# A hybrid attention block: q, k, v order, second q and k buffers, eight staging tiles for y and product banks for the turned probabilities in its differential heads

## The chip, the cores and the metric

The kernel runs on one core of a Trainium2 chip. The metric is the device time of one execution in microseconds (us); the median of the runs is given, beside the time of each. Five engines work side by side, each through its own queue of instructions in order: TensorE (PE in the profile; PEld is its weight load), VectorE (DVE), ScalarE (ACT), GpSimd (POOL) and SyncE (SP). SyncE issues most of the transfers, GpSimd some.

## The reference

One layer on 512 tokens and 16 learned ones ahead of them, width 1024, all in float32. Two attentions read the same normed input: a stick-breaking one with 8 heads of 128, and a differential one with 8 heads that have two maps of 64 each. Their outputs are projected, merged by gates, projected again and followed by a SwiGLU.

```python
def diff_attn_block(q, k, v, lam, slopes, qpos, kpos, qcid, kcid):
    s = jnp.einsum('bhcqd,bhckd->bhcqk', q, k).astype(jnp.float32) * (DF_HEAD_DIM ** -0.5)
    ...
    s = jnp.where(mask, s + bias[None, :, None], -jnp.inf)
    p = jax.nn.softmax(s, axis=-1)
    w = p[:, :, 0] - lam * p[:, :, 1]
    return jnp.einsum('bhqk,bhkd->bhqd', w.astype(v.dtype), v)
...
        y_sb = o_sb @ w_br_sb[l]
        y_df = o_df @ w_br_df[l]
        gates = jax.nn.sigmoid(xn @ w_gate[l] + b_gate[l]).reshape(B, L_pad, 2, D)
        merged = gates[:, :, 0] * y_sb + gates[:, :, 1] * y_df
        h = h + merged @ w_out[l]
```

## The kernel before

**Products.** Each float32 operand is split into a high part and a low part, and each product is three matmuls: high by high, high by low, low by high (L227, L228, L229, in `mm3`). The normed input lies transposed on chip as xT_h and xT_l. Results collect in PSUM: two tiles of two banks under the tag z (`z_tile`, L63) and four single banks under the tag mm (`mm_tile` and `tr_tile`, L57 and L60), which go round among the projections, y, the turns of v and the norm of a head.

**Weights.** They come in blocks of 512 KB. The list `stream` (L78 to L117) fixes their order; `stage_one` (L128) issues the load of the next block on SyncE into one of three staging tiles `wst` (L141, L144), and `split` (L74) makes the high part `wh` on ScalarE (L75) and the low part `wl` on VectorE (L76). `weights` (L215) prepares as many blocks ahead as `READY` says (3) in the stick-breaking heads and 2 later; `at_of["df", 0, 2]` marks where that changes.

**The heads.** The main loop (L921 to L955) runs 8 stick-breaking heads, then 8 differential ones. Each head is a generator that issues its scores, maps, turns and weighted values, and at each `yield n` the loop puts in up to n units of other work: projections of the next head, and the product `y` of a finished pair of heads with the branch's output weights. A y unit makes two of y's eight blocks (L711), twelve matmuls of 512 columns. The units of a head are those of its successor, then the first y unit, the turn of the successor's v (L462 to L478), and the second y unit. The scheduler places the instructions of these pieces by priority; evacuations and the last steps of a map carry a raised one (`EVAC`).

**A differential head** (`df_head`, L622). `scores` and `scores3` write two maps at a time to a z tile (L632, L633); VectorE adds the bias and takes the maximum (L636), ScalarE exponentiates (L660), VectorE normalises and subtracts the second map (L663 to L666), which leaves `pr`. Then `attn_out` (L482) turns the probabilities with transposes (L493, L507, L510), copies them out as a_h, a_l, a_f and a_s (L495, L496, L511, L514), and `weighted` multiplies by v ("av" below, L516 to L525). The result is copied off z (L690); its norm (L695) is left for the next head.

**q and k of a differential head** (`df_units`, L594). Both have one buffer per part, under the tags qh, ql, kh and kl. The evacuation splits each half of the partitions into its high and low parts (L604, L605 for q, L611, L612 for k), and for k two transfers on GpSimd's queue (L615) copy the finished half to the other partitions, 264 KB each. The units of a head run v, q, k (L618), and its weights come in that order too (L93).

**y and its way home.** Each y block is copied from its bank by ScalarE (L725) to a staging tile `ys`, one of two of that name alternately with `sg` tiles, or, for the last pair of differential heads, the tiles of the maps (L718 to L723), and stored in device memory by GpSimd, for a branch's first pair plainly, after that with addition (L727, L729). At the end `y_back` (L974) loads the sums on SyncE, and GpSimd multiplies them by the gates (L991).

**Shared memory.** The stick-breaking heads from the third on use token sums, in tA and tB. tA lies in the pool xtp under the tag y_sb; the residual rows `hres` (L997, four loads of 512 KB on GpSimd's queue, L999) use the same tag, so they may be loaded once tA was last read. tB lies in opool under the tag y_df.

Of the kernel before, what the change touches and what calls it, by code (L numbers as in the profile page):

```python
# [9 lines left out]
F32 = mybir.dt.float32  # L10
F32R = mybir.dt.float32r
# [5 lines left out]
P = 128  # L17
D = 1024
SEQ = 512
NM = 16  # L20
L = NM + SEQ
KT = D // P
# [13 lines left out]
STAGE, READY, START = 5, 3, 4  # L36
# [4 lines left out]
def block_kernel(ctx: ExitStack, tc: tile.TileContext, x, meta, norm_mix_g, w_in, w_gate, b_gate,  # L41
# [18 lines left out]
    def tr_tile():  # L60
        return ps_mm.tile([P, 512], F32, tag="mm", name="tr")

    def z_tile():  # L63
        return ps_z.tile([P, 2, 512], F32, tag="z", name="z")
# [25 lines left out]
        if h > 2:  # L90
            rows(("y_sb", h - 3), w_br_sb, (h + 1) % 2 * 512, (h - 3) // 2 * 2)
    for h in range(NH):
        for i in (2, 0, 1):  # L93
            cols(("df", h, i), w_in, (3 + i) * D + h * P)
        if h < 3:
            rows(("y_sb", h + 5), w_br_sb, (h + 1) % 2 * 512, (h + 5) // 2 * 2)
        else:
            rows(("y_df", h - 3), w_br_df, (h + 1) % 2 * 512, (h - 3) // 2 * 2)
# [20 lines left out]
    at_of = {c[0]: n for n, c in enumerate(stream)}  # L119
# [95 lines left out]
    def weights(key):  # L215
        at = at_of[key]
        if at < START:
            return loaded[key]
        if at >= first_ffn:
            return fpools["down"](key)  # L220
        prepare(prep_at[key] + (READY if at < at_of["df", 0, 2] else 2))
        return loaded[key]

    def mm3(ps, pairs, start=True, stop=True, skip=False):
# [42 lines left out]
    xT = (xT_h, xT_l)  # L267

    ydram = ctx.enter_context(tc.tile_pool(name="ydram", bufs=1, space=bass.MemoryType.DRAM))
    y_count = [0]  # L270

    tA = xtp.tile([P, 2, 2, 4, HL], F32R, tag="y_sb", name="tA")
    y_part = {n: [ydram.tile([P, SEQ], F32, name=f"{n}_{f}") for f in range(KT)] for n in ("y_sb", "y_df")}
# [205 lines left out]

        return kv_units(key, lambda ps, s: nc.scalar.copy(vT[:, s], ps)), turn  # L480

    def attn_out(blocks, d, lo_rows):  # L482

        qn = P - lo_rows
        off = (0, 512, 896)
        a_h = ap_.tile([P, 1152], F32R, tag="a_h", name="a_h")
        a_l = ap_.tile([P, 1152], F32R, tag="a_l", name="a_l")
        a_f = ap_.tile([P, P], F32, tag="a_f", name="a_f")

        def turn(j, pt):  # L490
            n = 512 - j * P
            for t in range(j, NQ):
                nc.tensor.transpose(pt[:, (t - j) * P:(t - j + 1) * P], blocks(t, j * P, (j + 1) * P), ident)  # L493
            c = slice(off[j], off[j] + n)
            nc.scalar.copy(a_h[:, c], pt[:, 0:n])  # L495
            nc.vector.tensor_tensor(a_l[:, c], pt[:, 0:n], a_h[:, c].bitcast(F32), op=ALU.subtract)  # L496

        def turn_first():
            z = z_tile()
            turn(0, z[:, 0])  # L500
            turn(1, z[:, 1])

        def turn_rest():
            z = z_tile()
            turn(2, z[:, 0])
            pt = z[:, 1]
            nc.tensor.transpose(pt[:, 384:512], blocks(3, 3 * P, 4 * P), ident)  # L507
            for t in range(NQ):
                b = blocks(t, (t + 1) * P - 32 * t, (t + 1) * P + NM)
                nc.tensor.transpose(pt[0:32 * t + NM, t * qn:(t + 1) * qn], b[lo_rows:P], ident[lo_rows:P, lo_rows:P])  # L510
            nc.scalar.copy(a_f, pt[:, 384:512])  # L511
            for t in range(NQ):
                r, c = slice(32 * t, 32 * t + NM), slice(t * qn, (t + 1) * qn)
                (nc.scalar.copy if t < 2 else nc.vector.tensor_copy)(a_s[r, c], pt[r, c])  # L514

        def weighted():  # L516
            vf, vh, vl = d["v"]
            ps = z_tile()[:, 0]
            for j in range(3):
                n = 512 - j * P  # L520
                mm3(ps[:, j * P:512], [(vh[:, j], vl[:, j], a_h[:, off[j]:off[j] + n], a_l[:, off[j]:off[j] + n])], j == 0, False)
            nc.tensor.matmul(ps[:, 3 * P:512], lhsT=vf[:, 0], rhs=a_f, start=False, stop=False)
            nc.tensor.matmul(ps.rearrange("p (t q) -> p t q", q=P)[:, :, lo_rows:P], lhsT=vf[:, 1],
                             rhs=a_s[:, 0:4 * qn], start=False, stop=True)
            return ps  # L525

        return turn_first, turn_rest, weighted
# [22 lines left out]
    def sb_head(h, d, o_h, o_l):  # L550
        qh, ql = d["q"]
        kh, kl = d["k"]
        zA, zB = z_tile(), z_tile()

        def score(o, t, k0, k1, mo, mn):
            q = slice(t * P, (t + 1) * P)
            mm3(o, [(qh[:, q], ql[:, q], kh[:, k0:k1], kl[:, k0:k1])], stop=(mn == 0))
            if mn:
                nc.tensor.matmul(o[:, mo:mo + mn], lhsT=ident_b, rhs=mask_b[:, 0:mn], start=False, stop=True)

        score(zA[:, 0, 0:256], 0, 0, 256, NM, P)
        score(zA[:, 0, 144:416], 1, 0, 272, NM + P, P)
        score(zA[:, 1, 0:416], 2, 0, 416, NM + 2 * P, 144)
        score(zB[:, 0, 0:HL], 3, 0, HL, 0, 0)
        score(zB[:, 1, 0:HL], 3, HL, L, 400 - HL, P)
        res = []
        for z, n in ((zA, 416), (zB, HL)):
            zz = z[:, :, 0:n]
            e = ap_.tile([P, 2, n], F32, tag=("w2" if n == 416 else "w1"), name="e")
            s = ap_.tile([P, 2, n], F32, tag=("w3" if n == 416 else "w0"), name="s")  # L570
            nc.scalar.activation(e, zz, AF.Abs)
            nc.scalar.activation(e, e, AF.Exp, scale=-1.0)
            nc.scalar.activation(e, e, AF.Ln, bias=1.0)
            nc.vector.scalar_tensor_tensor(s, zz, 0.0, e, op0=ALU.max, op1=ALU.add)
            sf = s.rearrange("p a b -> p (a b)")
            for a, b in (((0, 144), (144, 416), (416, 832)) if n == 416 else ((0, L),)):
                f = sf[:, a:b][:, ::-1]
                nc.vector.tensor_tensor_scan(f, f, f, 0.0, op0=ALU.add, op1=ALU.bypass)  # L578
            nc.vector.tensor_tensor(s, zz, s, op=ALU.subtract)
            nc.scalar.activation(s, s, AF.Exp)  # L580
            res.append(sf)
        base = ((0, 0), (0, 144), (0, 416), (1, 0))
        t1, t2, av = attn_out(lambda t, k0, k1: res[base[t][0]][:, base[t][1] + k0:base[t][1] + k1], d, 96)
        yield 4 if h + 1 < SEVEN else 5
        t1()
        yield 1
        t2()
        yield 1
        ps = av()
        nc.scalar.copy(o_h, ps)  # L590
        nc.vector.tensor_tensor(o_l, ps, o_h.bitcast(F32), op=ALU.subtract)


    def df_units(h):  # L594
        d = {}
        hs = (slice(0, 64), slice(64, 128))
        q = [ap_.tile([P, SEQ], F32R, tag=("qh", "ql")[c], name=f"dq{c}") for c in range(2)]
        k = [ap_.tile([P, 2, L], F32R, tag=("kh", "kl")[c], name=f"dk{c}") for c in range(2)]
        d["q"], d["k"] = q, k

        def q_evac(ps):
            for c in range(2):
                a, b = hs[c], hs[1 - c]
                nc.scalar.activation(q[c][a], ps[a], AF.Copy, scale=DF_SCALE)  # L604
                nc.vector.scalar_tensor_tensor(q[c][b], ps[a], DF_SCALE, q[c][a].bitcast(F32),  # L605
                                               op0=ALU.mult, op1=ALU.subtract)

        def k_evac(ps, s, scale):
            for c in range(2):
                a = hs[c]  # L610
                nc.scalar.activation(k[c][a, 0, s], ps[a], AF.Copy, scale=scale)  # L611
                nc.vector.scalar_tensor_tensor(k[c][a, 1, s], ps[a], scale, k[c][a, 0, s].bitcast(F32),  # L612
                                               op0=ALU.mult, op1=ALU.subtract)
                if s.stop == L:
                    nc.gpsimd.dma_start(k[c][hs[1 - c]].bitcast(F32), k[c][a].bitcast(F32))  # L615

        kv, turn = kv_all("df", h, k_evac, d)
        return d, kv[2:4] + halves(("df", h, 0), xT, QT, q_evac) + kv[0:2], turn  # L618

    late = []  # L620

    def df_head(h, d, o_h, o_l):  # L622
# [53 lines left out]
        yield 1  # L676
        scores3(1)
        maps(3)
        t1, t2, av = attn_out(lambda t, k0, k1: prs[t][:, 0, k0:k1], d, 64)
        yield 3 if h < NH - 1 else 2  # L680
        t1()
        yield 1
        t2()
        yield 2
        ps = av()
        of = ap_.tile([P, SEQ], F32, tag="of", name="of")
        sq = ap_.tile([P, SEQ], F32, tag="sq", name="sq")
# [21 lines left out]
    def y_units(name, i, o):  # L709

        def unit(fs):  # L711
            wh, wl = weights((name, i))
            for f in fs:
                ps = mm_tile()
                cs = slice(f % 4 * P, (f % 4 + 1) * P)
                mm3(ps, [(wh[:, k, cs], wl[:, k, cs], o[0][:, k], o[1][:, k]) for k in range(2)])

                if name == "y_df" and i > 5:  # L718
                    ys = ap_.tile([P, SEQ], F32, tag=f"w{y_count[0] % 4}", name="ys")
                elif y_count[0] % 2:  # L720
                    ys = ap_.tile([P, SEQ], F32, tag="ys", bufs=2, name="ys")
                else:
                    ys = gate_tile(0)  # L723
# [197 lines left out]
    for br in range(2):  # L921
        name, head = (("y_sb", sb_head), ("y_df", df_head))[br]
        if br:
            nc.gpsimd.memset(a_s, 0.0)
        for h in range(NH):
            if (br, h) == (0, 0):
                tB["t"] = opool.tile([P, 2, 2, 4, HL], F32R, tag="y_df", name="tB", bufs=1)
# [363 lines left out]
```

## Time and profile before

| | us |
|---|---|
| runs | 997.58, 999.05, 1001.49 |
| median | 999.05 |
| the profiled execution | 1000.49 |
| its span in the trace | 998.6 |
| TensorE busy | 970.5 (97%) |
| VectorE busy | 687.9 (69%) |
| ScalarE busy | 572.2 (57%) |
| GpSimd busy | 158.2 (16%) |

The mean granted TensorE clock is 0.993 of full speed. The rows shown further on have these forms. A wait: engine, tile and line, what it waited for, us in total, times, longest. A stretch: from and to, its length, busy time and instructions of PE, PEld, DVE, ACT and POOL, the granted clock, the busy share of the DMA engines, GB/s. A row of the timeline: start, duration, engine, line, operation, result and operands, count, and in brackets the idle time before it and what ended it. A group: line, engine, operation, count, busy us, mean ns of one. An issue of a transfer: count, KB, us from issue to landing.

### The profile page before, as it was taken

How to read it: one execution, taken by the hardware profiler on the slowest of the kernel's cores; microseconds unless marked ns; L12 is line 12 of the kernel's file. 1: busy time of each engine (PE TensorE's matmuls, PEld its weight loads, DVE VectorE, ACT ScalarE, POOL GpSimd, SP SyncE). 2: the span in 40 equal slices, each digit the busy share in tenths (PEclk: the TensorE clock that was granted, in tenths of full speed). 3: DMA queues.
4: the chain of work that ended last, by engine and by line, in shares of the span. 5: the costliest groups of instructions: out<-in, count | busy, mean ns of one | idle time of the engine just before them, and what ended most of it. 6: DMA issues, size and time to landing. Idle time of an engine off the chain costs nothing.

```text
span 998.6 us, 16211 instructions
## 1 busy us (share of the span) xinstructions
PE 970.5 (97%) x6213; PEld 870.4 (87%) x6213; DVE 687.9 (69%) x1244; ACT 572.2 (57%) x1091; POOL 158.2 (16%) x216
## 2 busy tenths in 40 slices
PE   7999999989999999999999999989999999999996
PEld 5998888879888998889878888879999999988885
DVE  8998678764567777678632633798888888754544
ACT  5676766665566666666772533575555555643533
POOL 4010112121232222322314530000000000000103
PEclk9999999998999999999999999999999999999999
DMA  7312444465563444643838732223343434332212
GB/s 214 86 43 65 127 131 96 97 190 127 127 142 105 93 129 128 148 109 92 161 84 209 223 117 85 85 78 114 94 118 94 119 90 122 100 112 99 92 43 85
DMA packets 140241, 114.12 MB, mean 114 GB/s; under 512 B 4962, under 2 KB 115715, under 8 KB 140163
## 3 DMA queue, kind: packets, MB, share of 16 engines
q1 hardware_dynamic: 129810, 89.29, 29.7%
q0 software_dynamic: 10192, 23.73, 11.9%
q8 instruction: 49, 0.80, 0.3%
q14 instruction: 30, 0.24, 0.1%
q10 hardware_dynamic: 160, 0.07, 0.0%
HBM read 89.87 MB, written 18.87 MB: 109 GB/s over the span
## 4 chain that ended last, share of the span: by engine, by line
PE 78%; DVE 8%; ACT 6%; DMA 5%; issue 2%; POOL 1%; SPq 0%; DVEq 0%; POOLq 0%; ACTq 0%
PE mm L229 18%; PE mm L227 18%; PE mm L228 18%; PE z L227 6%; PE z L229 6%; PE z L228 6%; DMA dk<-dk 3%; PE z L493 1%; ACT wh L75 1%; PE z L632 1%; DVE wl L76 1%; PE z L633 1%; DMA wst<-in_w_in_dram 1%; DVE s L578 1%; DMA xs<-in_x_dram 1%
## 5 line engine op out<-in xcount | busy, mean ns | idle before, releaser
L76 DVE TENSOR_TENSOR wl<-wst,wh 128x1024 fp32r<-128x1024 f32 (+1 forms) x150 | 170.0, 1137 | 118.9 <-ACT wh L75 118.7
L228 PE MATMUL mm<-xT_l,wh 128*128 128x264 f32 (+2 forms) x656 | 213.7, 326 | 2.2 <-DVE xT_l L828 2.2
L227 PE MATMUL mm<-xT_h,wh 128*128 128x264 f32 (+2 forms) x656 | 214.6, 327 | 0.6 <-ACT xT_h L827 0.6
L229 PE MATMUL mm<-xT_h,wl 128*128 128x264 f32 (+2 forms) x656 | 213.5, 325 | 0.0
L75 ACT CAST wh<-wst 128x1024 fp32r<-128x1024 f32 (+1 forms) x150 | 145.8, 972 | 98.9 <-PE mm L228 40.4
L228 PEld LDWEIGHTS mm<-xT_l,wh 128*128 128x128 f32 x656 | 124.2, 189 | 11.6 <-DVE xT_l L828 2.4
L227 PEld LDWEIGHTS mm<-xT_h,wh 128*128 128x128 f32 x656 | 124.4, 190 | 10.3 <-ACT xT_h L827 1.1
L229 PEld LDWEIGHTS mm<-xT_h,wl 128*128 128x128 f32 x656 | 124.1, 189 | 9.8
L228 PE MATMUL mm<-hT_l,wh 128*128 128x256 f32 x284 | 80.5, 284 | 0.7 <-DVE hT_l L1074 0.7
L227 PE MATMUL mm<-hT_h,wh 128*128 128x256 f32 x284 | 80.2, 284 | 0.6 <-DVE sg L1169 0.6
L229 PE MATMUL mm<-hT_h,wl 128*128 128x256 f32 x284 | 80.1, 283 | 0.0
L660 ACT ACTIVATE pr<-pr,nm 128x144 f32<-128x144 f32 (+3 forms) x64 | 36.3, 568 | 40.4 <-DVE nm L658 40.4
L228 PEld LDWEIGHTS mm<-hT_l,wh 128*128 128x128 f32 x284 | 53.7, 189 | 1.2 <-DVE hT_l L1074 1.1
L227 PEld LDWEIGHTS mm<-hT_h,wh 128*128 128x128 f32 x284 | 53.4, 189 | 1.1 <-DVE sg L1169 0.7
L229 PEld LDWEIGHTS mm<-hT_h,wl 128*128 128x128 f32 x284 | 53.6, 189 | 0.0
L227 PE MATMUL mm<-o_h,wh 128*128 128x512 f32 x128 | 52.3, 410 | 0.3 <-ACT o_h L703 0.3
L229 PE MATMUL mm<-o_h,wl 128*128 128x512 f32 x128 | 51.6, 404 | 0.0
L228 PE MATMUL mm<-o_l,wh 128*128 128x512 f32 x128 | 50.0, 392 | 0.0
L227 PE MATMUL mm<-t_h,wh 128*128 128x256 f32 x168 | 47.4, 282 | 1.3 <-ACT wh L75 1.0
L228 PE MATMUL mm<-t_l,wh 128*128 128x256 f32 x168 | 47.3, 281 | 1.1 <-DVE t_l L1089 1.1
L475 POOL COPY v_s<-vT 128x16 f32<-128x16 f32 x64 | 17.8, 307 | 190.6 <-ACT vT L480 82.3
L229 PE MATMUL mm<-t_h,wl 128*128 128x256 f32 x168 | 47.3, 281 | 0.0
(314 smaller groups left out, 2508.0 us busy)
## 6 DMA issues: line engine op xcount, KB each, us to landing
wst<-in_w_in_dram SPq DMA_DIRECT2D x40, 512.0 KB, 4.1
wst<-in_w_ffn_gate_dram SPq DMA_DIRECT2D x22, 512.0 KB, 3.7
wst<-in_w_ffn_down_dram SPq DMA_DIRECT2D x22, 512.0 KB, 3.5
wsu<-in_w_ffn_up_dram SPq DMA_DIRECT2D x21, 512.0 KB, 3.8
wst<-in_w_gate_dram SPq DMA_DIRECT2D x16, 512.0 KB, 4.6
y_df<-ys POOLq DMA_DIRECT2D x20, 256.0 KB, 6.2
dk<-dk POOLq DMA_DIRECT2D x16, 264.0 KB, 5.8
wst<-in_w_br_sb_dram SPq DMA_DIRECT2D x8, 512.0 KB, 4.9
```

What stands on the lines that cost most here:

```text
L75: (hi_copy or nc.scalar.copy)(hi, src)
L76: (lo_eng or nc.vector).tensor_tensor(lo, src, hi.bitcast(F32), op=ALU.subtract)
L227: nc.tensor.matmul(ps, lhsT=ah, rhs=bh, start=(start and i == 0), stop=False, skip_group_check=skip)
L228: nc.tensor.matmul(ps, lhsT=ah, rhs=bl, start=False, stop=False, skip_group_check=skip)
L229: nc.tensor.matmul(ps, lhsT=al, rhs=bh, start=False, stop=(stop and i == n - 1), skip_group_check=skip)
L475: nc.gpsimd.tensor_copy(v_s[:, 32 * t:32 * t + NM], vT[:, (t + 1) * P:(t + 1) * P + NM])
L493: nc.tensor.transpose(pt[:, (t - j) * P:(t - j + 1) * P], blocks(t, j * P, (j + 1) * P), ident)
L578: nc.vector.tensor_tensor_scan(f, f, f, 0.0, op0=ALU.add, op1=ALU.bypass)
L632: nc.tensor.matmul(o, lhsT=q[c][:, qs], rhs=k[c][:, 0, k0:k1], start=True, stop=False)
L633: nc.tensor.matmul(o, lhsT=q[c][:, qs], rhs=k[c][:, 1, k0:k1], start=False, stop=True)
L660: nc.scalar.activation(pr[:, c], pr[:, c], AF.Exp, bias=nm[:, c:c + 1], accum_out=ls[:, t, c:c + 1])
```

## The change

1. **Order.** The weights of a differential head are streamed as q, k, v, and its units run q, k, v. The mark in `weights` moves to the first block of the differential branch.
2. **Second q and k.** Odd heads hold q and k in one tile `dqk` in tB's memory; even heads keep the old tags.
3. **Staging for y.** From the first differential head on, y goes through the eight slots of one tile `y_out` in tA's memory. `hres` has the same tag, so its loads now come behind the last store out of `y_out`.
4. **Turned probabilities.** `attn_out` is given its banks. Stick-breaking heads pass the two halves of a z tile as before; differential heads pass two mm banks for each of the two turns.
5. **Units.** The last yield of a differential head ahead of av is 1 where it was 2, so the second y unit comes behind av.

```diff
-        for i in (2, 0, 1):
+        for i in range(3):
             cols(("df", h, i), w_in, (3 + i) * D + h * P)
...
-        prepare(prep_at[key] + (READY if at < at_of["df", 0, 2] else 2))
+        prepare(prep_at[key] + (READY if at < at_of["df", 0, 0] else 2))
...
-    def attn_out(blocks, d, lo_rows):
+    def attn_out(blocks, d, lo_rows, banks):
...
         def turn_first():
-            z = z_tile()
-            turn(0, z[:, 0])
-            turn(1, z[:, 1])
+            for j, pt in enumerate(banks()):
+                turn(j, pt)
 
         def turn_rest():
-            z = z_tile()
-            turn(2, z[:, 0])
-            pt = z[:, 1]
+            p2, pt = banks()
+            turn(2, p2)
...
-        q = [ap_.tile([P, SEQ], F32R, tag=("qh", "ql")[c], name=f"dq{c}") for c in range(2)]
-        k = [ap_.tile([P, 2, L], F32R, tag=("kh", "kl")[c], name=f"dk{c}") for c in range(2)]
+        if h % 2:
+
+            both = opool.tile([P, 4 * L + 2 * SEQ], F32R, tag="y_df", name="dqk", bufs=1)
+            q = [both[:, 4 * L + c * SEQ:4 * L + (c + 1) * SEQ] for c in range(2)]
+            k = [both[:, 2 * c * L:2 * (c + 1) * L].rearrange("p (a l) -> p a l", a=2) for c in range(2)]
+        else:
+            q = [ap_.tile([P, SEQ], F32R, tag=("qh", "ql")[c], name=f"dq{c}") for c in range(2)]
+            k = [ap_.tile([P, 2, L], F32R, tag=("kh", "kl")[c], name=f"dk{c}") for c in range(2)]
...
-        return d, kv[2:4] + halves(("df", h, 0), xT, QT, q_evac) + kv[0:2], turn
+        return d, halves(("df", h, 0), xT, QT, q_evac) + kv, turn
...
-        t1, t2, av = attn_out(lambda t, k0, k1: prs[t][:, 0, k0:k1], d, 64)
+        t1, t2, av = attn_out(lambda t, k0, k1: prs[t][:, 0, k0:k1], d, 64, lambda: (tr_tile(), tr_tile()))
         yield 3 if h < NH - 1 else 2
         t1()
         yield 1
         t2()
-        yield 2
+        yield 1
...
-
-                if name == "y_df" and i > 5:
-                    ys = ap_.tile([P, SEQ], F32, tag=f"w{y_count[0] % 4}", name="ys")
+                if y_out:
+                    ys = y_out[0][:, y_count[0] % KT]
...
             nc.gpsimd.memset(a_s, 0.0)
+            y_out.append(xtp.tile([P, KT, SEQ], F32, tag="y_sb", name="y_out"))
```

In the changed kernel the lines between L499 and L575 stand two further up and most behind them four or five further down: L505 and L508 are the old L507 and L510, L610 and L617 the old L605 and L612, L637 the old L632, L671 the old L666, L996 and L1004 the old L991 and L999.

Three places show how the instructions move. TensorE's queue at the second turn of the fifth differential head, where pr are the probabilities, o_h the heads' outputs in a y unit and vT, v_s the next head's v; before:

```order
L493 MATMUL z<-ident,pr 128x128 x5
L469 MATMUL tr<-ident,vT 128x128 x4
L476 MATMUL tr<-ident,v_s 128x128
L227 MATMUL mm<-o_h,wh 128x512
L228 MATMUL mm<-o_l,wh 128x512
L507 MATMUL z<-ident,pr 128x128
L510 MATMUL z<-ident,pr 16x64
L510 MATMUL z<-ident,pr 48x64
L510 MATMUL z<-ident,pr 80x64
L510 MATMUL z<-ident,pr 112x64
L229 MATMUL mm<-o_h,wl 128x512
```

and after:

```order
L493 MATMUL tr<-ident,pr 128x128 x2
L505 MATMUL tr<-ident,pr 128x128
L508 MATMUL tr<-ident,pr 16x64
L508 MATMUL tr<-ident,pr 48x64
L508 MATMUL tr<-ident,pr 80x64
L508 MATMUL tr<-ident,pr 112x64
L469 MATMUL tr<-ident,vT 128x128 x4
L476 MATMUL tr<-ident,v_s 128x128
L227 MATMUL z<-a_h,vh 128x512
L228 MATMUL z<-a_l,vh 128x512
L229 MATMUL z<-a_h,vl 128x512
```

All turns go to product banks, three of the old five transposes have moved up to the first turn, and av follows at once, where a y unit stood.

VectorE's queue from the last scores of that head (pr and mx with the bias) to the end of its last map (pr 128x528), and what follows; before:

```order
L636 ISA pr,mx<-z,bias 128x528
L636 ISA mx 128x1
L658 TENSOR_SCALAR nm<-mx 128x2
L663 RECIPROCAL rc<-ls 128x2
L664 TENSOR_TENSOR rc<-rc,cn 128x2
L665 TENSOR_SCALAR pr<-pr,rc 128x528
L666 SCALAR_TENSOR_TENSOR pr<-pr,rc 128x528
L605 SCALAR_TENSOR_TENSOR dq_4466<-mm,dq_4466 64x512
L76 TENSOR_TENSOR wl<-wst,wh 128x1024
L605 SCALAR_TENSOR_TENSOR dq_4467<-mm,dq_4467 64x512
L612 SCALAR_TENSOR_TENSOR dk_4468<-mm,dk_4468 64x264
L612 SCALAR_TENSOR_TENSOR dk_4469<-mm,dk_4469 64x264
```

and after:

```order
L641 ISA pr,mx<-z,bias 128x528
L641 ISA mx 128x1
L671 SCALAR_TENSOR_TENSOR pr<-pr,rc 128x400
L617 SCALAR_TENSOR_TENSOR dqk<-mm,dqk 64x264
L663 TENSOR_SCALAR nm<-mx 128x2
L76 TENSOR_TENSOR wl<-wst,wh 128x1024
L617 SCALAR_TENSOR_TENSOR dqk<-mm,dqk 64x264
L668 RECIPROCAL rc<-ls 128x2
L669 TENSOR_TENSOR rc<-rc,cn 128x2
L617 SCALAR_TENSOR_TENSOR dqk<-mm,dqk 64x264
L670 TENSOR_SCALAR pr<-pr,rc 128x528
L671 SCALAR_TENSOR_TENSOR pr<-pr,rc 128x528
```

The low parts of the next head's q and k, and a weight split, stand ahead of the end of the last map, where they stood behind it.

GpSimd's queue at the residual's loads; before, in the seventh stick-breaking head (v_s are columns of v, y_sb_80 and on the blocks of y):

```order
L729 DMA y_sb_87<-ys 128x512
L475 COPY v_s<-vT 128x16
L999 DMA hres<-in_x_dram 128x1024 x4
L475 COPY v_s<-vT 128x16 x3
L729 DMA y_sb_80<-sg 128x512
L729 DMA y_sb_81<-ys 128x512
```

and after, behind the last differential head:

```order
L733 DMA y_df_92<-y_out 128x512
L996 TENSOR_TENSOR sg<-sg,y_df 128x512
L733 DMA y_df_93<-y_out 128x512
L996 TENSOR_TENSOR sg<-sg,y_df 128x512
L733 DMA y_df_94<-y_out 128x512
L733 DMA y_df_95<-y_out 128x512
L1004 DMA hres<-in_x_dram 128x1024 x2
L996 TENSOR_TENSOR sg<-sg,y_sb 128x512
L1004 DMA hres<-in_x_dram 128x1024 x2
```

The loads have moved behind the last stores of y_df, and the merges with the gates stand between those stores.

More of the change, by code (lines that the diff above doesn't have):

```diff
@@ L269, in block_kernel @@
     ydram = ctx.enter_context(tc.tile_pool(name="ydram", bufs=1, space=bass.MemoryType.DRAM))
-    y_count = [0]
+    y_count, y_out = [0], []
     tA = xtp.tile([P, 2, 2, 4, HL], F32R, tag="y_sb", name="tA")
@@ L582, in sb_head @@
         base = ((0, 0), (0, 144), (0, 416), (1, 0))
-        t1, t2, av = attn_out(lambda t, k0, k1: res[base[t][0]][:, base[t][1] + k0:base[t][1] + k1], d, 96)
+        t1, t2, av = attn_out(lambda t, k0, k1: res[base[t][0]][:, base[t][1] + k0:base[t][1] + k1], d, 96,
+                              lambda: (lambda z: (z[:, 0], z[:, 1]))(z_tile()))
         yield 4 if h + 1 < SEVEN else 5
```

## The prediction

> **What bounds the kernel now.** The page first: part 1 for the engines, part 4 for the chain that ended last.
>
> ```profile
> PE 970.5 (97%) x6213; PEld 870.4 (87%) x6213; DVE 687.9 (69%) x1244; ACT 572.2 (57%) x1091; POOL 158.2 (16%) x216
> PE 78%; DVE 8%; ACT 6%; DMA 5%; issue 2%; POOL 1%; SPq 0%; DVEq 0%; POOLq 0%; ACTq 0%
> ```
>
> TensorE is busy 97% of 998.6 us, and the change takes no matrix product away. So the most that it can gain is TensorE's idle time, and the time in which its clock was low, in the stages that it touches. The second view is therefore TensorE's waits between 225 and 525 us, which hold the end of the stick-breaking heads and all differential heads; the columns are us in total, times, longest. The rows of PEld are waits of the weight load ahead of a matmul.
>
> ```profile
> PE z L507 <- DVE a_l L496: 2.7, 1, 2.7
> PE z L632 <- DMA dk<-dk: 2.2, 6, 0.6
> PE z L493 <- DVE a_l L496: 1.4, 4, 0.4
> PEld z L493 <- DVE a_l L496: 3.6, 8, 0.7
> PEld z L632 <- DMA dk<-dk: 2.5, 5, 0.6
> ```
>
> Three waits, and each has its own part of the change: one long one, and two that come back in every head.
>
> **A: the long wait.** The stretches around it (length, PE, PEld, DVE, ACT and POOL busy, granted clock, share of the DMA engines, GB/s):
>
> ```profile
> 205.00:215.00 10.00, 10.00 (x65) 9.06 (x64) 8.97 (x13) 5.18 (x9) 2.38 (x5) 1.00 0.70 236
> 215.00:222.00 7.00, 6.92 (x46) 5.87 (x44) 2.56 (x4) 3.36 (x5) 0.00 (x0) 1.00 0.87 273
> 222.00:225.00 3.00, 0.38 (x1) 0.18 (x1) 3.00 (x6) 2.18 (x4) 1.66 (x4) 0.84 0.04 13
> 225.00:231.00 6.00, 6.00 (x25) 5.53 (x25) 1.52 (x4) 1.88 (x6) 1.41 (x2) 0.51 0.96 216
> ```
>
> TensorE does nothing for most of 222 to 225, and then works six us at a clock of 0.51. What it waited for, from the timeline and the chain of waits, with the times of the transfers from the page's part 6 below:
>
> ```profile
> 208.75 0.57 POOL L999 DMA_DIRECT2D hres<-in_x_dram  x1 [2.34 <-PE mm L229]
> 213.30 7.11 DMA wst<-in_w_in_dram
> 220.49 1.05 ACT L75 CAST wh<-wst 128x1024 fp32r<-128x1024 f32 x1 [3.29 <-DMA wst<-in_w_in_dram]
> 224.62 0.47 PE L507 MATMUL z<-ident,s 128*128 128x128 f32 x1 [2.70 <-DVE a_l L496]
> wst<-in_w_in_dram SPq DMA_DIRECT2D x40, 512.0 KB, 4.1
> hres<-in_x_dram POOLq DMA_DIRECT2D x4, 512.0 KB, 5.1
> dk<-dk POOLq DMA_DIRECT2D x16, 264.0 KB, 5.8
> ```
>
> The last token sums are done, their memory is free, and the residual rows, whose tile shares it, are fetched at once: four loads of 512 KB from 208.75 on. A weight block issued at 213.30 then takes 7.11 us where 4.1 is the median. ScalarE stands 3.29 us for it, the k evacuation, the lo part and a_l queue behind the split on ScalarE and VectorE, and TensorE stands 2.70.
>
> In the changed kernel y's staging tile takes that memory for the differential branch, so hres is loaded only after the last y store. The weight block meets no 2 MB of other loads and lands 7.11 − 4.1 = 3.0 us earlier, which is more than the 2.70. The half clock is worth 6.0 × (1 − 0.51) = 2.9. Upper end 2.7 + 2.9 = 5.6; lower end 2.7, should the clock drop anyway; I take 5.2, near the upper, because the drop follows the only such wait in the window directly. The dearer half rests on the clock: the row is a wait of 2.70 and then 0.51. The Trainium skill, TensorE: Matmul & The Clock Gate, section What's actually happening, has the array fall to half clock after an idle window of about 3.4 us; a gap of 2.7 would not be one, and by that rule A would be 2.7 alone. The trace shows the drop all the same, though not its cause.
>
> **B: q and k of the next head.** A differential head repeats every 30.9 us. Two of the seven rows, the first scores of the first head, and the second copy of the head from 386.91:
>
> ```profile
> 294.10:325.05 30.95, 30.60 (x200) 27.54 (x199) 22.39 (x56) 19.74 (x46) 9.31 (x14) 1.00 0.52 118
> 386.91:417.84 30.93, 30.54 (x201) 27.52 (x199) 22.91 (x56) 19.73 (x46) 8.90 (x14) 1.00 0.42 109
> 263.88 0.36 PE L632 MATMUL z<-dk,dq 128*128 128x256 f32 x1 [0.57 <-DMA dk<-dk]
> 264.67 0.39 PE L632 MATMUL z<-dk,dq 128*128 128x256 f32 x1 [0.32 <-DMA dk<-dk]
> 412.46 0.52 POOL L615 DMA_DIRECT2D dk<-dk  x1 [0.17 <-issue]
> ```
>
> Before, the two copies of k's halves between partitions come last in a head, since units run v, q, k and the single buffers hold k's evacuation until the last scores of the head have read the old k; the scores then wait for a copy of 5.8 (the last row: issued 25.6 us into a head that lasts 30.9). Now units run q, k, v with a second q and k for odd heads. The rest of the v units, the turns, the weighted values and both y units then stand between the copies' issue and their use. By an estimate from the durations of a head's instructions in the new order they are issued some 18.2 us into a head and land by 18.2 + 5.8 = 24, at most 26; the next scores come at 29.5 to 30. Cover at least 3.5 us, so the wait goes. It costs 2.2 by the rows of PE, 2.2 + 2.5 = 4.7 if PEld's came besides; I take the middle, 3.5.
>
> The second buffers lie in tB's memory, last read by the token sums, so nobody waits for it. The weights' order only swaps equal 512 KB blocks: nothing.
>
> **C: the turned probabilities.** Before, the second turn writes the other half of the same z tile that the first one's a_l still reads (L493), so TensorE stands for VectorE. Now each turn has a product bank of its own. The bounds are 1.4 and 1.4 + 3.6 = 5.0; a few of these waits lie in the last stick-breaking heads, whose z tiles stay as they were, so 3.0. The four extra banks per head come from the rotation of four that projections, y and the v turns use. Each of them is read by one or two copies and free again one y unit later, so I take them as no cost, up to 0.3 a head where a copy is late. One more thing: scores now follow four y products instead of av, so av's copy off z is done in time; below 0.5 in all.
>
> **New waits.** VectorE's last map must be ready for the first turn. Before (timeline of VectorE and TensorE in the head from 386.91, then groups of that head):
>
> ```profile
> 389.78 1.28 DVE L658 TENSOR_SCALAR nm<-mx 128x2 f32<-128x2 f32 x1
> 395.12 0.15 DVE L658 TENSOR_SCALAR nm<-mx 128x2 f32<-128x2 f32 x1
> 396.68 0.17 DVE L663 RECIPROCAL rc<-ls 128x2 f32<-128x2 f32 x1 [0.68 <-ACT pr L660]
> 402.78 0.17 DVE L663 RECIPROCAL rc<-ls 128x2 f32<-128x2 f32 x1 [1.62 <-ACT pr L660]
> 403.71 0.77 DVE L666 SCALAR_TENSOR_TENSOR pr<-pr,rc 128x528 f32<-128x528 f32 x1
> 407.74 0.38 PE L493 MATMUL z<-ident,pr 128*128 128x128 f32 x2
> L612 DVE SCALAR_TENSOR_TENSOR dk<-mm,dk 64x264 fp32r<-64x264 f32 x4 | 1.7, 430 | 0.5 <-ACT dk L611 0.5
> L605 DVE SCALAR_TENSOR_TENSOR dq<-mm,dq 64x512 fp32r<-64x512 f32 x2 | 1.4, 689 | 0.1
> L76 DVE TENSOR_TENSOR wl<-wst,wh 128x1024 fp32r<-128x1024 f32 x5 | 6.1, 1226 | 5.2 <-ACT wh L75 5.2
> ```
>
> The map ended at 404.48, 17.6 into the head, and the turn came at 20.8: 3.3 of cover. Now q's two lo parts (1.4), k's four (1.7) and two more weight splits (2.4) stand ahead of the last map: 17.6 + 5.5 = 23.1 at the worst. VectorE idles 0.68 + 1.62 = 2.3 for exponentials in that stretch, and the work that moves in fits there; the scores start about 0.7 earlier without their own wait (4.7 over seven heads): 20.1. The slow L658 of 1.28, where later ones take 0.15, coincides with GpSimd's squares; av now comes a y unit ahead of the scores, so that is likely gone too: 18.6 to 19.0. TensorE's work ahead of the turn is unchanged, and without its wait ends at 20.1. Cover between 0 and 1.5: thin. I put 1.5 us on all heads together for this and the banks, between 0 and 4.0 (0.6 a head).
>
> **D: the tail.** The stores of y_df, the loads that read y back and the gates' products end the branch; now hres comes behind the last store.
>
> ```profile
> 517.66 0.73 PE L227 MATMUL mm<-o_h,wh 128*128 128x512 f32 x2 [0.31 <-ACT o_h L703]
> 541.84 1.28 POOL L991 TENSOR_TENSOR sg<-sg,y_sb 128x512 f32<-128x512 f32 x1 [9.35 <-DMA y_sb<-y_sb]
> 520.00:560.00 40.00, 40.00 (x178) 33.14 (x177) 14.96 (x14) 14.75 (x23) 19.46 (x16) 1.00 0.81 202
> 560.00:640.00 80.00, 80.00 (x366) 66.19 (x366) 36.33 (x57) 33.20 (x57) 14.45 (x8) 1.00 0.35 110
> 613.98 2.05 DVE L1031 TENSOR_TENSOR hres<-hres,z 128x512 f32<-128x512 f32 x3 [1.73 <-PE z L229]
> ```
>
> TensorE is 40.00 of 40.00 busy here, while GpSimd stands 9.35 for y_sb. In the new order the y_sb merges stand between the last stores on GpSimd's queue, and hres's four loads of about 5.1 go out, by an estimate from the stores' and merges' rows, some 27 us after the last y units begin at 517.66, about 545. By 560 to 565 they have landed, and the first sum that reads hres starts at 613.98, in a stretch where the DMA engines are 0.35 busy: some 50 us to spare, price 0.
>
> **Sum.** 5.2 + 3.5 + 3.0 + 0.2 (the copy off z) − 1.5 = 10.4. The profiled execution took 1000.49 and would take 990.1; the median of the runs is 999.05, 1.44 below it, so 988.65, called 988.7.
>
> **Rivals.**
> 1. *The clock drops there anyway*, or the weight block is late for another reason, so A gives 2.7 or less. For it: the wait is the end of a chain of five queued steps. Against: the slow weight load of this stretch stands under hres. 988.7 + 2.5 = 991.2.
> 2. *hres, moved, collides in the tail.* From 520 to 560 the DMA engines are already 0.81 busy; 2 MB more there delay a gate's weights as they did at 213: 2.7 + 2.9 and a little for the gates' own order, say 6.3, so 995.0. Against it: TensorE did not wait once in those 40 us, although the DMA engines were as busy there. The Trainium skill, DMA: Bandwidth & Descriptors, section Issuing engines are not separate DMA queues, says that transfers of all issuing engines interleave on the same 16 engines; the row of 7.11 against 4.1 agrees, so GpSimd's own queue is no shelter.
> 3. *The dk and a_l waits only move to the turn*, the map being later by as much: B and C give nothing, and 988.7 + 6.5 = 995.2. For it: cover of 0 to 1.5 only.
> 4. *VectorE becomes the bound of a head: slower.* The idle 2.3 and the early start do not help, because ScalarE too has q's and k's casts ahead of its exponentials. The map then ends at 23.1 and the turn waits 23.1 − 20.1 = 3.0 a head, in seven heads 21: 999.05 − 11.9 (the sum without new waits) + 21 = 1008.2, more if the clock drops after each. It decides from 11.9 / 7 = 1.7 a head on and passes 0.5% at (11.9 + 5) / 7 = 2.4. Against it: VectorE is busy 22.9 of 30.93 and its idle time now lies where this work goes.
>
> **How the numbers follow.** A measurement of this kernel can tell about 0.5%, 5 us, from no change: faster is below 994.05, slower above 1004.05. Chances: the forecast 0.67, rival 1 0.09, rival 2 0.08, rival 3 0.09, rival 4 0.07. Bounds of the sum: upper ends 5.6 + 4.7 + 5.0 + 0.5 = 15.8, so 983.2; lower ends 2.7 + 2.2 + 1.4 − 4.0 = 2.3, so 996.8. The range is 983 to 996.5, which takes in rivals 1 to 3 and leaves out rival 4 and the corners. Rivals 2 and 3 lie just past the edge, in no change: faster 0.67 + 0.09 and 0.02 of their milder cases, 0.78; same 0.15; slower 0.07.
>
> **What would show it.** Right: no wait at L505 near 222 and no low clock behind it; the wst load there at about 4; no dk row among TensorE's waits; head periods of about 30.0 instead of 30.9; the hres loads past 540. Wrong: a wait for pr at the first turn, periods at 30.9 or above, a wait for wh or wl between 540 and 580.

## The result, and the profile after

The changed kernel takes 988.29 us (median of four runs, 987.56 to 989.00), the kernel before 998.86 beside it. The ratio is 0.9898, with a 95% interval from 0.988 to 0.9916: 1.0% faster, 10.6 us. The profiled execution took 988.8, with a span of 987.0. From its page, the engines and the chain that ended last:

```profile
PE 963.9 (98%) x6213; PEld 869.3 (88%) x6213; DVE 675.5 (68%) x1244; ACT 572.6 (58%) x1091; POOL 166.4 (17%) x216
PE 88%; DVE 6%; ACT 4%; DMA 1%; issue 1%; POOL 0%; SPq 0%; DVEq 0%; ACTq 0%; POOLq 0%
```

TensorE's share of the chain has risen from 78% to 88%, and the transfers' has fallen from 5% to 1%. TensorE's waits between 220 and 525 us, those of the matmuls and then of the weight loads:

```profile
PE z L493 <- DVE a_l L496: 1.3, 1, 1.3
PE mm L228 <- DVE o_l L709: 0.3, 1, 0.3
```

```profile
PEld z L493 <- DVE a_l L496: 1.7, 2, 1.6
PEld tr L508 <- issue: 1.3, 8, 0.2
PEld mm L228 <- DVE o_l L709: 0.6, 1, 0.6
```

No row names dk, and the one large wait for a_l is in the last stick-breaking head. The stretches of the old long wait, and the loads' splits on ScalarE there:

```profile
215.00:222.00 7.00, 7.00 (x48) 6.25 (x47) 5.36 (x8) 4.48 (x7) 0.86 (x1) 1.00 0.73 219
222.00:225.00 3.00, 3.00 (x17) 2.20 (x16) 2.55 (x6) 2.13 (x7) 1.33 (x4) 1.00 0.57 168
225.00:231.00 6.00, 6.00 (x39) 5.23 (x39) 1.63 (x3) 3.45 (x8) 1.73 (x2) 1.00 1.01 190
```

```profile
214.79 1.48 SPq L144 DMA_DIRECT2D wst<-in_w_in_dram  x2
218.87 1.05 ACT L75 CAST wh<-wst 128x1024 fp32r<-128x1024 f32 x1 [0.18 <-DMA wst<-in_w_in_dram]
```

TensorE is busy all the time at full clock. The block issued at 214.79 is split from 218.87 on, so it landed within 4.1 us. ScalarE waits 0.18 for it, where it waited 3.29. A differential head, then in it the end of the last map, the second copy of k, the first turn and the next scores (VectorE, GpSimd, TensorE):

```profile
379.93:409.96 30.03, 30.03 (x200) 27.51 (x199) 21.10 (x55) 19.72 (x47) 9.94 (x14) 1.00 0.48 124
398.75 0.77 DVE L671 SCALAR_TENSOR_TENSOR pr<-pr,rc 128x528 f32<-128x528 f32 x1
398.49 0.52 POOL L620 DMA_DIRECT2D dqk<-dqk  x1 [0.43 <-DVE dqk L617]
400.12 0.93 PE L493 MATMUL tr<-ident,pr 128*128 128x128 f32 x7
409.95 0.28 PE L637 MATMUL z<-dqk 128*128 128x256 f32 x1
```

The head lasts 30.03 us and TensorE is busy for 30.03 of it. The map ends at 399.52, 0.6 ahead of the turn. The copy is issued 18.6 us into the head, some 11 ahead of the scores. The tail:

```profile
507.00:550.00 43.00, 43.00 (x191) 35.56 (x190) 15.43 (x16) 18.09 (x27) 22.47 (x21) 1.00 0.97 257
532.71 1.13 POOL L1004 DMA_DIRECT2D hres<-in_x_dram  x2 [4.87 <-DMA y_df<-y_out]
```

hres now goes out at 532.71 into DMA engines that are 0.97 busy, and TensorE does not wait.

Where the 11.6 us between the two spans came from follows from the first scores of the first and the eighth differential head, before and after:

```profile
263.88 0.36 PE L632 MATMUL z<-dk,dq 128*128 128x256 f32 x1 [0.57 <-DMA dk<-dk]
480.33 0.35 PE L632 MATMUL z<-dk,dq 128*128 128x256 f32 x1 [0.30 <-DMA dk<-dk]
```

```profile
260.25 0.28 PE L637 MATMUL z<-dk,dq 128*128 128x256 f32 x1
470.02 0.28 PE L637 MATMUL z<-dqk 128*128 128x256 f32 x1
```

Ahead of the heads 3.6 us were gained, over seven heads (480.33 − 263.88) − (470.02 − 260.25) = 6.7, and behind that 1.3. Of the 1.3, 1.0 lies in the eighth head itself, up to the first product of the last y units (516.51 before, 505.17 after).

The part ahead holds an accident of the execution. At the start of the kernel, which the change does not touch, the clock was low over one more stretch in the changed kernel's trace (before, then after):

```profile
20.00:30.00 10.00, 8.48 (x70) 7.97 (x69) 8.45 (x25) 4.87 (x13) 2.07 (x3) 1.00 0.34 97
```

```profile
20.00:30.00 10.00, 7.78 (x53) 7.52 (x53) 8.44 (x24) 4.06 (x11) 2.03 (x2) 0.83 0.35 102
```

So the changed kernel's trace stood 1.5 us later when the weight block went out (214.79, where it was 213.30). From there to the first scores it gained 3.6 + 1.5 = 5.1: in this pair of executions the long wait and the low clock behind it are gone together.

### The profile page after: what moved, and what is told of

It reads as the page before. It is cut to its first block, busy times and chain, and to the rows that moved or that the text cites. A ratio compares the mean times of both kernels' runs of the same rounds, so it can differ in the third digit from the quotient of the medians.

```text
span 987.0 us, 16198 instructions
## 1 busy us (share of the span) xinstructions
PE 963.9 (98%) x6213; PEld 869.3 (88%) x6213; DVE 675.5 (68%) x1244; ACT 572.6 (58%) x1091; POOL 166.4 (17%) x216
## 4 chain that ended last, share of the span: by engine, by line
PE 88%; DVE 6%; ACT 4%; DMA 1%; issue 1%; POOL 0%; SPq 0%; DVEq 0%; ACTq 0%; POOLq 0%
PE mm L229 20%; PE mm L227 20%; PE mm L228 20%; PE z L227 6%; PE z L229 6%; PE z L228 6%; PE z L638 1%; PE z L637 1%; PE tr L493 1%; PE tr L469 1%; PE z L493 1%; ACT wh L75 1%; DVE s L576 1%; PE z L521 1%; DVE wl L76 0%
## 5 line engine op out<-in xcount | busy, mean ns | idle before, releaser
L641 DVE CUSTOM_DVE_ANT_0 pr<-z,bias 128x144 f32<-128x144 f32 (+3 forms) x64 | 30.9, 502 | 34.9 <-PE z L638 34.8
L475 POOL COPY v_s<-vT 128x16 f32<-128x16 f32 x64 | 26.3, 440 | 162.5 <-DVE vT L405 78.2
L1260 POOL TENSOR_TENSOR outs<-hres,gF 128x512 f32<-128x512 f32 x4 | 5.1, 1291 | 262.2 <-DVE hres L1036 261.3
```

What stands on the lines that cost most here:

```text
L475: nc.gpsimd.tensor_copy(v_s[:, 32 * t:32 * t + NM], vT[:, (t + 1) * P:(t + 1) * P + NM])
L641: nc.vector.tensor_tensor_reduce(po, zz, bb, scale=1.0, scalar=-3.0e38, op0=ALU.add, op1=ALU.max, accum_out=mx[:, t, c:c + 1])
```

## The experiments

**The long wait: the transfers alone.** The first two kernels keep the whole change and put traffic back where hres was loaded before, into the still unused y_out. The data are dead, and y overwrites them.

```diff
             y_out.append(xtp.tile([P, KT, SEQ], F32, tag="y_sb", name="y_out"))
+            dead = y_out[0].rearrange("p (t a) s -> p t (a s)", a=2)
+            for t in range(4):
+                nc.gpsimd.dma_start(dead[:, t], xv[:, t])
```

> The changed kernel, with one thing added: as y's staging tile is born, the four residual loads of 512 KB go into it (dead data, overwritten by y), so the 2 MB stand in GpSimd's queue where hres stood before. Theory (the transfers delay a weight block, TensorE waits for it, the clock drops after): the long wait of about 2.7 us near 222 and the half clock behind it come back, 988.3 + 5.6 = 993.9. Rival (the wait went because y's staging or the order changed, whatever the transfers do): 988.3, no wait there.

It took 990.73, a ratio of 0.9925 (0.9908 to 0.9942) to the kernel before. Its chain of waits, stretches and timeline at the place:

```profile
213.87 6.42 DMA wst<-in_w_in_dram
222.00:225.00 3.00, 0.97 (x8) 0.42 (x6) 3.00 (x6) 2.19 (x4) 1.71 (x4) 1.00 0.07 25
225.00:231.00 6.00, 6.00 (x37) 5.29 (x34) 2.15 (x5) 3.31 (x10) 1.93 (x3) 1.00 1.02 223
224.53 0.33 PE L505 MATMUL z<-ident,s 128*128 128x128 f32 x1 [2.03 <-DVE a_l L496]
```

The slow load and the wait are back; the half clock is not. The transfers are the cause of the wait. The median is 2.4 above the changed kernel's, not 5.6: the wait is 2.0 here, and the clock's part is missing in this execution.

The second kernel has `range(2)`.

> As the run with four dead loads, but two of them (1 MB). Theory: the weight block is late by about half, 1.5 us; the long wait was 2.7 us for a delay of 3.0, so 0 to 1.2 us of wait are left and no half clock: 988.3 to 989.5. Rival (any collision there costs the clock): 992 or more.

It took 989.06 (ratio 0.9907). TensorE is busy 2.97 of the three us, so half of the traffic costs no wait:

```profile
222.00:225.00 3.00, 2.97 (x21) 2.62 (x21) 1.51 (x3) 1.10 (x4) 1.76 (x2) 1.00 0.99 201
```

**The long wait: y's staging.** Part 3 undone in the changed kernel (the old staging for y, no `y_out`; this diff), and part 3 alone in the kernel before (the same lines the other way, and the empty list `y_out`):

```diff
-                if y_out:
-                    ys = y_out[0][:, y_count[0] % KT]
+                if name == "y_df" and i > 5:
+                    ys = ap_.tile([P, SEQ], F32, tag=f"w{y_count[0] % 4}", name="ys")
...
-            y_out.append(xtp.tile([P, KT, SEQ], F32, tag="y_sb", name="y_out"))
```

> The changed kernel with part 3 undone: y goes through the old staging tiles, and hres is loaded early as before. Theory: only the long wait and its half clock come back, 988.3 + 5.6 = 993.9, and the differential heads keep their period of 30.03 us. Rival (the eight staging tiles also free the differential heads): the heads get slower too, 0.3 us or more each, and the time passes 996.

> The kernel before with part 3 alone: y's eight staging tiles in tA's memory, so that hres comes late; the order, the buffers and the turned probabilities stay. Theory: the long wait and the half clock go, 998.9 - 5.6 = 993.3, and the period of a differential head stays at 30.9. Rival (the parts only work together): 997 or more.

The first took 990.79 (ratio 0.9927, 0.9911 to 0.9944), the second 995.88 (0.9974, 0.9963 to 0.9985). Both say the same of part 3: (0.9927 − 0.9898) × 999 = 2.9 us, and (1 − 0.9974) × 999 = 2.6, with an interval from 1.5 to 3.7. The dead loads cost as much, (0.9925 − 0.9898) × 999 = 2.7. Neither kernel moves the period of a differential head (table below), so part 3 works through hres alone. It is worth 2.6 to 2.9, not 5.6.

The traces account for the gap, most of it by the clock. Five more of them hold the wait, of 1.8 to 2.1 us where the kernel before had 2.7, and the stretch behind it was slow in two of the five (order and buffers alone and banks alone, below, both 0.72). One with the drop (order and buffers alone) and one without (part 3 undone):

```profile
225.00:231.00 6.00, 6.00 (x28) 5.38 (x27) 1.76 (x5) 2.41 (x9) 0.97 (x2) 0.72 1.08 223
```

```profile
225.00:231.00 6.00, 6.00 (x37) 5.29 (x36) 2.25 (x5) 3.19 (x10) 1.92 (x3) 1.00 1.05 226
```

By an estimate from the six traces that hold the wait, it lasts 2.0 on average, and the low clock behind it costs (2.9 + 1.7 + 1.7) / 6 = 1.0, from 6.0 × (1 − 0.51) once and 6.0 × (1 − 0.72) twice. That makes 3.1, near the 2.6 to 2.9 of the medians.

A low clock comes behind shorter waits too. Near 655 us, in work that the change does not touch, each of the fourteen traces has one wait of 1.1 and one of about 1.0. In five of them the clock behind these is 0.69 to 0.72 over five us, in the others it stays at 1.00. The last stick-breaking head with product banks (last experiment), then the changed kernel:

```profile
655.00:660.00 5.00, 4.75 (x29) 4.46 (x29) 3.31 (x6) 1.32 (x4) 0.13 (x1) 0.71 0.76 242
```

```profile
655.00:660.00 5.00, 4.10 (x32) 3.90 (x33) 4.68 (x8) 2.79 (x6) 0.59 (x1) 1.00 0.70 219
```

So two executions can differ by 5 × (1 − 0.71) = 1.5 us there with no part of the change behind it, and the length of a wait alone does not say whether the clock drops.

**The differential heads: three parts, together and apart.** Order (with second buffers), banks and the place of the second y unit were tried in all eight combinations, counting the two kernels. These are the edits that undo one part in the changed kernel: banks, order, unit, and then the buffers.

```diff
-        t1, t2, av = attn_out(lambda t, k0, k1: prs[t][:, 0, k0:k1], d, 64, lambda: (tr_tile(), tr_tile()))
+        t1, t2, av = attn_out(lambda t, k0, k1: prs[t][:, 0, k0:k1], d, 64, lambda: (lambda z: (z[:, 0], z[:, 1]))(z_tile()))
```

> The changed kernel with part 4 undone: the turned probabilities go to the halves of a z tile again. Theory (a_l waits cost 3.0 in the sum): the second turn waits for a_l again, 0.4 a head, 988.3 + 3.0 = 991.3, between 989.7 and 993.3. Rival (the position of the units alone took the a_l waits away): 988.3.

```diff
-        for i in range(3):
+        for i in (2, 0, 1):
...
-        prepare(prep_at[key] + (READY if at < at_of["df", 0, 0] else 2))
+        prepare(prep_at[key] + (READY if at < at_of["df", 0, 2] else 2))
...
-        return d, halves(("df", h, 0), xT, QT, q_evac) + kv, turn
+        return d, kv[2:4] + halves(("df", h, 0), xT, QT, q_evac) + kv[0:2], turn
```

> The changed kernel with part 1 undone: order v, q, k, second buffers kept. Theory (the order sets when the copies of k are issued, and y's place behind av gives them 2.8 us more): the copies are issued late again, some 23 us into a head, and land at about 29, just at the scores: 988.3 to 990. Rival (the order alone is what counts): the dk waits come back in full, 988.3 + 3.5 = 991.8 or more.

```diff
         t2()
-        yield 1
+        yield 2
         ps = av()
```

> The changed kernel with part 5 undone: both y units ahead of av, the scores right behind it. Theory (the y unit behind av covers av's copy off z and the squares on GpSimd; without it the run with order and buffers alone showed 2.0 us of waits for the copy and 2.0 for the squares over seven heads): 988.3 + 2 to 4 = 990.3 to 992.3. Rival (a matter of the order alone): 988.3.

```diff
-        if h % 2:
...
-        else:
-            q = [ap_.tile([P, SEQ], F32R, tag=("qh", "ql")[c], name=f"dq{c}") for c in range(2)]
-            k = [ap_.tile([P, 2, L], F32R, tag=("kh", "kl")[c], name=f"dk{c}") for c in range(2)]
+        q = [ap_.tile([P, SEQ], F32R, tag=("qh", "ql")[c], name=f"dq{c}") for c in range(2)]
+        k = [ap_.tile([P, 2, L], F32R, tag=("kh", "kl")[c], name=f"dk{c}") for c in range(2)]
```

> The changed kernel with part 2 undone: one q and k per part, order q, k, v kept. In the trace of the changed kernel the last scores of a head are done some 11.5 us into it, and the next q is finished at about 8, k at 14 to 20. Theory (the order is what brings the copies of k forward, the second buffers only let q's evacuation start 3 us sooner): 988.3 to 990.0, no dk row. Rival (without second buffers the evacuations hold product banks and VectorE's queue): 992 or more, with waits for banks among TensorE's.

The same edits of the change itself, one at a time, in the kernel before (the lines are those of the diff above): parts 1 and 2, part 4, part 5.

> The kernel before with parts 1 and 2 alone: order q, k, v and second buffers. Theory: the dk rows go, 998.9 - 3.5 = 995.4, less what new waits at the turn take (0 to 1.5). Rival (the waits only move to the turn): 998 or more, with pr among TensorE's waits.

> The kernel before with part 4 alone: turned probabilities in product banks. Theory: the a_l rows go, the dk rows and the long wait stay, 998.9 - 3.0 = 995.9. Rival (a dk wait takes up what the a_l wait gives back, since the copies are issued at the same time as before): 998 or more.

> The kernel before with part 5 alone: the second y unit behind av. Theory (parts need each other): av's copy off z no longer delays the scores, some 0.2 a head, but the second turn's copies lose their cover, and the dk and a_l waits stay: 997.5 to 999. Rival (this move is the larger part of what the differential heads gained): 995 or less.

The period is a fifth of the time from the first scores of the second differential head to those of the seventh, read from each trace's timeline. The ratio is that of the whole kernel to the kernel before.

| kernel | order | banks | unit | second head | seventh head | period | median | ratio (95%) |
|---|---|---|---|---|---|---|---|---|
| before | - | - | - | 294.12 | 448.76 | 30.93 | 998.86 | 1 |
| order and buffers | x | - | - | 292.47 | 446.69 | 30.84 | 997.90 | 0.9985 (0.9969 to 1.0001) |
| banks | - | x | - | 294.75 | 452.94 | 31.64 | 1004.50 | 1.005 (1.0031 to 1.0069) |
| unit | - | - | x | 290.07 | 442.64 | 30.51 | 995.52 | 0.996 (0.9945 to 0.9976) |
| unit undone | x | x | - | 289.66 | 442.53 | 30.57 | 992.07 | 0.993 (0.9913 to 0.9947) |
| banks undone | x | - | x | 290.59 | 443.43 | 30.57 | 991.74 | 0.9929 (0.9909 to 0.9949) |
| order undone | - | x | x | 289.41 | 444.31 | 30.98 | 994.86 | 0.9956 (0.9942 to 0.9969) |
| changed | x | x | x | 289.80 | 439.99 | 30.04 | 988.29 | 0.9898 (0.988 to 0.9916) |
| buffers undone | x | x | x | 289.10 | 439.27 | 30.03 | 988.52 | 0.9888 (0.9869 to 0.9906) |
| part 3 undone | x | x | x | 291.17 | 441.34 | 30.03 | 990.79 | 0.9927 (0.9911 to 0.9944) |
| part 3 alone | - | - | - | 288.51 | 443.23 | 30.94 | 995.88 | 0.9974 (0.9963 to 0.9985) |

The rows with something undone have part 3 as well (but for its own row), so their ratios compare with 0.9898; the rows of single parts lack it and compare with 1. The row "order undone" keeps the second buffers.

Read in pairs, the unit gains 0.27 to 0.66 us a head whatever the other two do. Order and banks gain only together. With the banks the order is worth 1.07 and 0.94 a head, without them 0.09 and −0.06. The banks gain 0.27 and 0.53 in the new order, and lose 0.71 and 0.47 in the old one.

Against the expectations: banks undone (991.3 expected), unit undone (990.3 to 992.3) and buffers undone (988.3 to 990.0) came out as the theory had it. Order and buffers alone came out near the rival's 998, but not for its reason, since no row names pr. Banks alone were expected faster by the theory and unchanged by the rival, and are slower by 0.5%. The unit alone came out near the rival's 995, and not at the theory's 997.5 to 999. With the order undone the theory's 988.3 to 990 failed: the time passes the rival's 991.8, but behind the first head no dk row is left, and the time goes to waits for banks that neither named.

Waits show why the parts do not add. Banks alone, between 255 and 525 us:

```profile
PE mm L227 <- ACT sg L723: 2.9, 7, 0.4
PE mm L227 <- DVE dk L610: 1.4, 6, 0.2
PE z L630 <- DMA dk<-dk: 0.9, 2, 0.7
```

With the order v, q, k the projections next to the turns are k's, whose banks come free only after ScalarE and VectorE have split them, and the turns take four more banks of the same rotation. So y's products stand for a bank (the copy of an earlier y block, L723, and k's lo part, L610). Banks alone make a head 0.7 us slower. The same row is there with the order undone, where ScalarE's split of k stands ahead of the turn's copies and of y's (ScalarE, then TensorE):

```profile
PE mm L227 <- ACT y_out L729: 2.8, 7, 0.4
403.92 0.39 ACT L616 ACTIVATE dqk<-mm 64x264 fp32r<-64x264 f32 x1
405.11 0.59 ACT L729 COPY y_out<-mm 128x512 f32<-128x512 f32 x1
405.75 0.50 PE L227 MATMUL mm<-o_h,wh 128*128 128x512 f32 x1 [0.42 <-ACT y_out L729]
```

Order and buffers alone, weight loads between 255 and 525 us:

```profile
PEld z L493 <- DVE a_l L496: 4.2, 8, 1.0
PEld z L507 <- DVE a_l L496: 2.4, 8, 0.3
PEld z L638 <- ACT of L696: 2.0, 7, 0.3
PEld tr L703 <- POOL sql L76: 2.0, 7, 0.3
```

The dk rows are gone, as forecast, but other rows have grown in their place: the turns in z wait longer for a_l, the scores now stand for the copy of av off z (L696), and the norm for the squares. Part 5 removes the last two. With it undone in the changed kernel they are back:

```profile
PEld z L637 <- ACT of L695: 2.4, 7, 0.4
PEld tr L702 <- POOL sql L76: 2.0, 7, 0.3
```

Banks remove the first two. With the banks undone the a_l row stands at

```profile
PEld z L493 <- DVE a_l L496: 3.6, 8, 0.5
PEld z L227 <- DVE a_l L496: 1.7, 7, 0.2
```

Part 5 alone also shortened the head, by 0.4, and of the dk rows before about half were left:

```profile
PE z L632 <- DMA dk<-dk: 1.1, 3, 0.5
PEld z L632 <- DMA dk<-dk: 1.2, 3, 0.7
```

The second buffers give nothing in the new order: without them the heads keep their 30.03, and no wait for q, k or a bank comes up. That expectation held.

**The wait that is left.** The last stick-breaking head with product banks too, since the changed kernel waits for a_l there:

```diff
-                              lambda: (lambda z: (z[:, 0], z[:, 1]))(z_tile()))
+                              (lambda: (tr_tile(), tr_tile())) if h == NH - 1 else lambda: (lambda z: (z[:, 0], z[:, 1]))(z_tile()))
```

> The changed kernel, and the last stick-breaking head turns its probabilities in product banks too. Its trace shows one wait of 1.4 us for a_l at that head's second turn. Theory (it has the cause that the banks removed elsewhere): the wait goes, 988.3 - 1.4 = 986.9. Rival (VectorE is behind there with the next head's q and k, so the wait only moves, or banks run short): 988.3 or more.

It took 989.30 (ratio 0.9896, 0.9878 to 0.9914): no gain. The wait moved to a bank that holds a part of v:

```profile
PE mm L227 <- ACT vT L480: 1.2, 1, 1.2
```

No kernel here is faster than the changed one by more than the intervals can tell.

## Why the prediction was right, and where its terms were not

The forecast was 988.7 and the result 988.29. The sum of 10.4 was close to the measured 10.6 by luck: the heads gave about 2.5 more than their terms, and A 2.3 to 2.6 less, so that two misses cancelled.

- **A, 5.2 forecast, 2.6 to 2.9 measured.** The chain (hres, slow weight block, wait) was right and is shown by the dead loads. The size was not: "the drop follows the only such wait in the window directly" took one execution's wait and half clock for a price paid each time. The wait was 1.8 to 2.1 in the five other traces that hold it, and two of them show the drop. The lower end of 2.7, given for "should the clock drop anyway", was near the value, though the changed kernel's clock did not drop. The Trainium skill, TensorE: Matmul & The Clock Gate, section What's actually happening, says that the window is free-running, so that the same kernel shows a different number of slow matmuls at its start from run to run. The traces agree as to the start (1.00 and 0.83 from 20 to 30 us). What decides in a single execution whether the clock drops behind a wait is left open, and the row of before alone could not show that it is not paid each time.
- **B, 3.5 forecast.** The dk rows went to nothing, and the copies were issued 18.6 us into a head where 18.2 was said. But the working treated their time as free once the wait was gone. With order and buffers alone the head gains 30.93 − 30.84 = 0.09. Other waits were right behind, and the prediction did not ask of this part by itself what was late next. The second buffers, which the prediction took as half of the mechanism, do nothing here.
- **C, 3.0 forecast.** With order and unit in place the banks are worth 30.57 − 30.04 = 0.53 a head, 3.7 in seven; that size is near. But "free again one y unit later, so I take them as no cost" holds only with the new order: in the old one they cost 31.64 − 30.93 = 0.71 a head.
- **The copy off z, 0.2 forecast ("below 0.5 in all").** This step failed outright. Part 5 is worth 30.57 − 30.04 = 0.53 a head, 3.7 in seven, and 0.42 alone. In the kernel before the copy's row is small, and it grew to 2.0 when the wait for k was gone (order and buffers alone); the row for the squares, also 2.0 there, was not priced:

```profile
PEld z L632 <- ACT of L690: 0.5, 3, 0.2
```

- **New waits, 1.5 forecast, none measured.** The cover at the first turn was 0.6 in the head shown, within "between 0 and 1.5"; TensorE is busy 30.03 of 30.03. Rivals 3 and 4 fall with it. Rival 1, by which A gives 2.7 or less, had that term's size, but not its reason: in the changed kernel the block is not late and the clock there is 1.00.
- **D, 0 forecast and measured**, with hres at 532.71 where 545 − 11 = 534 would stand for a kernel that much earlier. The sign "past 540" did not take this off, and so was not met. Rival 2 falls: 0.97 of the DMA engines busy, and no wait.
- **The bound.** "TensorE's idle time, and the time in which its clock was low" was called the most that the change can gain. For a head that is too little: TensorE idled 30.95 − 30.60 = 0.35 and 30.93 − 30.54 = 0.39 in the two shown, at full clock, and the period fell by 0.89. The rest came off its busy time, which is now 30.03: the rows of PEld, which the terms B and C counted at their upper ends, would lie in that time, but no row shows it directly.

Seven heads gave 6.7 and the eighth 1.0, so the heads together gave 7.7 where the terms B, C, copy and new waits made 5.2, and A gave 2.6 to 2.9 where 5.2 stood. Together that is 10.3 to 10.6, the whole of the measured 10.6. The heads' part is read from one execution of each kernel.

## What to carry to other kernels

When several small waits end on the same few instructions, price the parts in order and ask after each what is late next: here two of three parts were worth next to nothing or less alone, and all three together 0.9 us a head. Before putting more work on a rotation of banks, look at which evacuation holds the banks next to it; the order of the projections decided whether the extra banks gained 0.3 to 0.5 us a head or lost 0.5 to 0.7. A drop of the clock behind a wait, seen in one execution, is a chance and not a price.

## What the runs showed of the hardware

Transfers on GpSimd's queue slowed those on SyncE's: a weight block of 512 KB took 7.11 us beside 2 MB, 6.42 beside the same 2 MB put back as dead data, where the median was 4.1; beside 1 MB TensorE had no wait. Waits of TensorE of 1.8 to 2.7 us were followed by a granted clock of 0.51 (the kernel before, 2.7) or 0.72 (order and buffers, 1.8) over the next six us, and in other executions by 1.00 (2.03 in the kernel with the dead loads). Two waits of about 1 us near 655 were followed by 0.69 to 0.72 over five us in five of fourteen traces, and by 1.00 in the others.
